# Two output projections as 2x2 block products by multiplication, with their weights' sums made by accumulating transfers

## The chip, the cores and the metric

The kernel runs on one NeuronCore of one Trainium2 chip. It is one program for five engines with an instruction queue each: TensorE (PE in the profile; its weight loads are PEld), VectorE (DVE), ScalarE (ACT), GpSimd (POOL) and SyncE (SP). Sixteen DMA engines move data between the chip's DRAM and the core's on-chip memory; in this kernel SP issues most transfers and POOL the rest. The metric is the device time of one execution in microseconds (us), given as the median of the runs.

## The reference, cut to what matters

An encoder layer is applied to two sequences of 1024 rows, `x_prompt` (b = 0 below) and `x_sample` (b = 1), all widths 1024:

```python
xn = rmsnorm(x, g_pre)
fv, fg, hv, hg, mg = split(xn @ w_in)           # 1024, 1024, 3*1024, 1024, 2*1024 columns
fz  = fftn(fv by groups).real
y_f = (fz * silu(fg)) @ w_fourier_out           # the F projection
z   = two long convolutions by FFT, gated, of short_conv(hv)
y_h = (z * silu(hg)) @ w_hyena_out              # the H projection
g_f, g_h = split(sigmoid(mg + b_merge))
out = (g_f * y_f + g_h * y_h) @ w_out
y   = x + rmsnorm(out, g_post)
```

The change concerns `y_f`, `y_h` and how their gated sum reaches the product with `w_out`.

## The kernel before

**Pairs.** A float32 number x is kept as a pair of rounded numbers h + l. `split` (L167) makes one: ScalarE casts x to h (L170) and VectorE, or POOL in places, subtracts h from x (L180). A product of pairs is three matmuls, h·h, h·l and l·h (`mm3`, `times`; all at L193). One matmul takes a 128x128 left factor and a 128x512 right factor.

**Stages.** `phase_fourier` (0 to about 200 us of the span) norms both inputs, spills the normed x to DRAM as `d_x` (L360) and does the Fourier branch. `phase_main` makes the filters' spectra (to about 700 us) and calls `branches` (L1030, to about 1677 us): per column tile `conv`, `conv_front`, `conv_back`, all of b = 0 before all of b = 1. `inproj` (L836) is its matmul with a 128-column tile of `w_in`: it loads 512 columns of weights at a time on SP, splits them with POOL (`wl<-wr,wh`, with two buffers for the raw weights and three for a pair), and for b = 0 keeps the pairs in DRAM by POOL's queue (`d_w`) so that b = 1 can load them. `load_x` (L823) loads a sequence's normed x in 8 tiles of 512 KB and splits each 1024 wide; it runs for b = 1 at about 1090 us. Ten gates of b = 1 (list `PLAIN`) are done plainly at the end of the stage.

`phase_gates` (L1118, 1677 to 1884 us) makes the other gates of b = 1 in 11 jobs. A job is two column tiles, that is a 2x2 block product done with seven products instead of eight (Winograd's form): the left factors are blocks 11, 12, 22 and sums s1 to s4 of the weights, the right factors blocks B11, B21, B22 and sums T1 to T4 of x. Each of the seven products is 12 matmuls (4 k-tiles of three). Results go to DRAM as `d_g`.

`phase_out` (L1230, 1884 to 2235 us) does F and H in four units, a unit being half of the rows of one sequence. A unit runs `project` (L1269) for F over 8 output tiles `dt` and then for H over 8: 24 matmuls each into one PSUM bank, with the left factor from `weight` (L1255), which loads 128x512 weights on POOL's queue (`wr<-in_w_fo`, `wr<-in_w_ho`) and splits them, again in each unit. `operand` loads the right factors (`sf`, `sh`), `gated` (L1288) multiplies a result by a sigmoid gate (L1293) loaded from `d_g`. F's gated results stay on chip (`yf`); H's are added to them and the sum is stored as `d_m` (L1377), in an order that later lets a 128x512 block be read in one piece. `beside` splits `w_out` and its sums between the units, half of the sums by way of DRAM (`d_t`).

`last_rows` (L1388, 2235 us to the end) multiplies `d_m` by `w_out` in 8 jobs of seven products, with the same Winograd form, norms the rows, adds x and stores y.

**What sets the order.** Each engine runs its own queue in order. A scheduler orders each queue; an instruction that depends on nothing may be moved far ahead of where it is written. `issue_after(i)` keeps what is written under it behind instruction i. Data that the program writes to DRAM and reads back, and buffers that rotate, are tracked: a reader waits for the transfer that wrote it, and a new use of a buffer for the last use of the old one.

Of the kernel before, what the change touches and what calls it, by code (L numbers as in the profile page):

```python
# [9 lines left out]
F32 = mybir.dt.float32  # L10
# [6 lines left out]
P = 128  # L17
D = 1024
# [142 lines left out]
class K:  # L161
# [34 lines left out]
    def setup(self, ctx):  # L196
# [29 lines left out]
        self.d_m = [dt(f"d_m{u}", [P, 4, 8, P]) for u in range(2 * NB)]  # L226
        self.d_t = [dt(f"d_t{j}", [P, 4, 512]) for j in range(2)]
# [595 lines left out]
    def load_x(self, b, ks=range(8)):  # L823
        nc = self.nc
        if 0 in ks:
            self.xh, self.xl = [], []
        for k in ks:
            h = self.xp.tile([P, L], F32R, tag=f"xh{k}", name=f"xh{b}_{k}", bufs=1)
            l = self.xp.tile([P, L], F32R, tag=f"xl{k}", name=f"xl{b}_{k}", bufs=1)
            r = l.bitcast(F32)  # L830
            nc.sync.dma_start(r, self.d_x[b][k])
            self.split(h, l, r, "dve", "act")
            self.xh.append(h)
            self.xl.append(l)

    def inproj(self, sec, mt, b=None):  # L836
# [3 lines left out]
        for q in range(2):  # L840
# [5 lines left out]
            if b:  # L846
                for t, k in zip(parts, kept):
                    nc.sync.dma_start(t.bitcast(F32), k[:, s])
            else:
                r = self.wp.tile([P, 512], F32, tag="w", name="wr", bufs=2)  # L850
                nc.sync.dma_start(r, a["w_in"][sec, mt][:, s])
                self.split(*parts, r, "pool", "act")
                if kept:
                    for t, k in zip(parts, kept):
                        nc.gpsimd.dma_start(k[:, s], t.bitcast(F32))
            for n in range(2):
                for kk in range(4):
                    k = 4 * q + kk
                    s = slice(512 * n, 512 * n + 512)
                    self.mm3(ps[:, s], (h[:, kk], l[:, kk]), (self.xh[k][:, s], self.xl[k][:, s]), k == 0, k == 7)  # L860
# [122 lines left out]
    def phase_main(self, nct=8, nb=NB, nf=16):  # L983
        tc, nc, a = self.tc, self.nc, self.a
        with ExitStack() as es:
# [19 lines left out]
            nc.gpsimd.tensor_copy(self.cfwd[:, 0, 0:1], self.xl[4][:, 0:1])  # L1005
# [6 lines left out]
            for i in range(nf):  # L1012
# [11 lines left out]
                if i in (2, 4, 6):  # L1024

                    s = slice((2, 4, 6).index(i) * INVW // 3, ((2, 4, 6).index(i) + 1) * INVW // 3)
                    nc.gpsimd.dma_start(self.cinv[:, :, s], a["c_inv"][:, :, s])
            self.branches(nb, nct, ws)

    def branches(self, nb, nct, ws):  # L1030
# [13 lines left out]
        def front(i):  # L1044
            b, n, c = steps[i]
# [72 lines left out]
    def phase_gates(self):  # L1118

        tc, nc, a = self.tc, self.nc, self.a
        wp, b = self.wp, 1
        jobs = [(s, c) for c in range(0, 8, 2) for s in (0, 4, 5, 6) if (s, c) not in self.PLAIN]
        with ExitStack() as es:
            pool = lambda n: es.enter_context(tc.tile_pool(name=n, bufs=1, reuse_waits="tile"))
            self.open_mm(es, "psg")
            gs, gw, gr = pool("gs"), pool("gw"), pool("gr")
            def prepare(sec, c):


                r = gr.tile([P, 4, 512], F32, tag="raw", name="wraw", bufs=2)
                for i in range(2):
                    nc.gpsimd.dma_start(r[:, 2 * i:2 * i + 2].rearrange("p a b -> p (a b)"), a["w_in"][sec, c + i])
                s = gw.tile([P, 4, 512], F32, tag="sum", name="wsum", bufs=1)
                A = {}

                def parts(n, pool, tags, src, bufs):
                    h, l = [pool.tile([P, 4, P], F32R, tag=t, name=t, bufs=bufs) for t in tags]
                    self.split(h.rearrange("p a b -> p (a b)"), l.rearrange("p a b -> p (a b)"), src, "dve", "act")  # L1140
                    A[n] = h, l
                parts("11", wp, ("wh", "wl"), r[:, 0], 3)
                parts("12", wp, ("wh", "wl"), r[:, 1], 3)
                self.add("dve", s[:, 0:2], r[:, 2].unsqueeze(1).to_broadcast([P, 2, 512]), r[:, 3::-3])
                self.add("dve", s[:, 2], s[:, 0], r[:, 0])
                parts("s2", gw, ("s2h", "s2l"), s[:, 2], 1)
                h, l = [gw.tile([P, 2, 4, P], F32R, tag=t, name=t, bufs=1) for t in ("s13h", "s13l")]
                f = lambda t: t.rearrange("p s a b -> p s (a b)")
                self.split(f(h), f(l), s[:, 0:2], "dve", "act")
                A["s1"], A["s3"] = (h[:, 0], l[:, 0]), (h[:, 1], l[:, 1])  # L1150
                self.add("dve", s[:, 3], s[:, 2], r[:, 1])
                parts("s4", gw, ("s4h", "s4l"), s[:, 3], 1)
                parts("22", gw, ("a2h", "a2l"), r[:, 3], 1)
                return A

            A = prepare(*jobs[0])
            TH, TL = [], []
            for k in range(4):
                r = gr.tile([P, 4, 512], F32, tag="raw", name="xraw", bufs=2)
                for i in range(2):  # L1160
                    nc.sync.dma_start(r[:, 2 * i:2 * i + 2].rearrange("p a b -> p (a b)"), self.d_x[b][k + 4 * i])
                s = gw.tile([P, 4, 512], F32, tag="sum", name="xsum", bufs=1)
                self.sums(s, r)
                h, l = [gs.tile([P, 4, 512], F32R, tag=f"{t}{k}", name=f"{t}{k}", bufs=1) for t in ("th", "tl")]
                self.split(h, l, s, "dve", "act")
                TH.append(h)
                TL.append(l)
            own = lambda k, n: (slice(0, 512), slice(512, 1024))[n]
            block = lambda i, n: [(self.xh[4 * i + k][:, own(k, n)], self.xl[4 * i + k][:, own(k, n)]) for k in range(4)]
            B11, B21, B22 = block(0, 0), block(1, 0), block(1, 1)  # L1170
            T1, T2, T3, T4 = [[(TH[k][:, j], TL[k][:, j]) for k in range(4)] for j in range(4)]

            def out(sec, c, n, p, q, op):

                s = slice(512 * n, 512 * n + 512)
                t = wp.tile([P, 512], F32, tag="gt", name="gt", bufs=3)
                if q is not None:
                    self.tt("dve", t, p, q, op)
                if sec in (0, 4):
                    f = gw.tile([P, 512], F32, tag="f", name="fz", bufs=3)  # L1180
                    nc.sync.dma_start(f, (self.d_sh if sec else self.d_fz)[b][c][:, s])
# [4 lines left out]
                nc.sync.dma_start(self.d_g[b][sec][c][:, s], t)  # L1186

            def kept(p, own=False, last=False):
                if own or last:
                    t = gw.tile([P, 512], F32, tag="u" if own else "f", name="u" if own else "v", bufs=1 if own else 3)  # L1190
                else:
                    t = wp.tile([P, 512], F32, tag="w", name="m", bufs=2)
                copied = nc.scalar.copy(t, p)
                if own:
                    self.copied = copied
                return t

            def first(A):
                pa, pb = self.psum("mm", 4, "pg"), self.psum("X", 2, "pg")
                self.times(pa, A["11"], B11, True)  # L1200
                m1 = kept(pa)
                self.times(pb, A["12"], B21, True)
                return pa, pb, m1
            pa, pb, m1 = first(A)
            for i, (sec, c) in enumerate(jobs):
                out(sec, c, 0, pb, m1, ADD)
                self.times(pa, A["s2"], T2, False)
                u = kept(pa, True)
                pc = self.psum("T", 2, "pg")
                self.times(pc, A["s3"], T3, True)  # L1210
                self.times(pa, A["s1"], T1, False)
                v = kept(pa, last=i + 1 == len(jobs))
                out(sec, c + 1, 1, pc, v, SUB)
                last = (A, pa, pc, u)
                if i + 1 < len(jobs):
                    A = prepare(*jobs[i + 1])
                    pa, pb, m1 = first(A)
                A_, pa_, pc_, u = last
                if i + 1 < len(jobs):
                    self.times(pa_, A_["s4"], B22, False)  # L1220
                    out(sec, c, 1, pa_, None, None)
                else:
                    pd = self.psum("X", 2, "pg")
                    self.times(pd, A_["s4"], B22, True)
                    out(sec, c, 1, pd, v, ADD)
# [392 lines left out]
```

## Time and profile before

| | us |
|---|---|
| runs | 2398.54, 2398.01, 2397.57 (median 2398.01) |
| profiled execution, span from first to last instruction | 2394.9 |
| F and H projections (`pyf`, `pyh`) on the chain | 1884 to 2235.5 |
| gates (`pg`) on the chain | 1677 to 1884 |
| last rows (`po`) | 2235.5 to the end |

The median of the runs is 3.1 us above the span of the profiled execution. The profile gives each engine's busy time, the chain of waits (from the last instruction back to whatever released each step), groups of equal instructions with count, busy time and mean, and the transfers with the time from issue to landing. In a group's line, `out<-in` names the tiles, and what follows the last bar is the engine's idle time just before these instructions and what ended it.

### The profile page before, as it was taken

What the parts mean: (1) busy time and instruction counts of PE and PEld (TensorE: products, weight loads), DVE (VectorE), ACT (ScalarE), POOL (GpSimd) and SP (SyncE); (2) the same over time, 40 slices, a digit from 0 to 9 for tenths busy, and PEclk for the clock granted to TensorE, in tenths of its full rate; (3) what the DMA queues carried; (4) which work ended last, traced back from release to release, by engine and by line L of the source; (5) the groups of instructions that cost most, each with busy time, mean ns of one, the idle gap of its engine ahead of it and who ended that gap; (6) DMA issues with size and microseconds to landing.
All of it is one profiled execution on the core that took longest, in us unless ns stands there. A gap on an engine that the chain in (4) does not pass through costs nothing.

```text
span 2394.9 us, 36369 instructions
## 1 busy us (share of the span) xinstructions
PE 2360.9 (99%) x12988; PEld 2053.6 (86%) x12988; DVE 1889.5 (79%) x3397; ACT 1084.2 (45%) x2063; POOL 461.6 (19%) x506
## 2 busy tenths in 40 slices
PE   6999999999999999999999999999999999999998
PEld 5998888888888888888888888888888888888887
DVE  7875787888879999999989999985555456665677
ACT  6654666677643333333322223333443445444444
POOL 3341222222232233230000000023000111112111
PEclk9999999999999999999999999999999999999999
DMA  8636655555665555545444444435544667776553
GB/s 264 219 129 220 204 169 165 171 171 159 204 215 177 172 170 187 176 145 203 150 131 133 137 150 133 143 121 198 165 160 141 211 215 259 251 259 213 166 166 132
DMA packets 221007, 428.33 MB, mean 179 GB/s; under 512 B 23254, under 2 KB 80952, under 8 KB 220570
## 3 DMA queue, kind: packets, MB, share of 16 engines
q1 hardware_dynamic: 193037, 333.03, 43.1%
q0 software_dynamic: 27568, 92.94, 11.5%
q8 instruction: 102, 1.67, 0.3%
q14 instruction: 79, 0.65, 0.1%
q10 hardware_dynamic: 221, 0.04, 0.0%
HBM read 290.12 MB, written 135.79 MB: 178 GB/s over the span
## 4 chain that ended last, share of the span: by engine, by line
PE 94%; DVE 2%; DMA 1%; ACT 1%; issue 1%; POOL 0%; DVEq 0%; ACTq 0%; POOLq 0%; SPq 0%
PE pin L193 41%; PE pg L193 8%; PE pyf L193 7%; PE pyh L193 7%; PE pX L193 7%; PE pT L193 7%; PE po L193 6%; PE pXf L193 3%; PE pfv L193 3%; PE pft L193 1%; PE tph L901 1%; DVE eo L180 0%; PE pQ L193 0%; DMA wr<-in_w_fo 0%; PE pse L193 0%
## 5 line engine op out<-in xcount | busy, mean ns | idle before, releaser
L193 PE MATMUL pin<-xh,wl 128*128 128x512 f32 x1440 | 563.2, 391 | 0.0
L193 PE MATMUL pin<-xl,wh 128*128 128x512 f32 x1440 | 562.8, 391 | 0.1
L193 PE MATMUL pin<-xh,wh 128*128 128x512 f32 x1440 | 561.9, 391 | 0.0
L180 POOL TENSOR_TENSOR wl<-wr,wh 128x512 fp32r<-128x512 f32 x132 | 227.6, 1725 | 1148.7 <-ACT wh L170 1125.4
L193 PEld LDWEIGHTS pin<-xl,wh 128*128 128x128 f32 x1440 | 271.0, 188 | 50.8 <-DVE xl L180 0.4
L193 PEld LDWEIGHTS pin<-xh,wh 128*128 128x128 f32 x1440 | 270.8, 188 | 51.0
L193 PEld LDWEIGHTS pin<-xh,wl 128*128 128x128 f32 x1440 | 271.0, 188 | 50.5
L170 ACT CAST wh<-wr 128x512 fp32r<-128x512 f32 x260 | 161.1, 620 | 333.6 <-PE pin L193 107.8
L180 DVE TENSOR_TENSOR t<-pX,k 128x1024 f32<-128x1024 f32 x128 | 155.6, 1216 | 9.8 <-PE pX L193 6.5
L193 PE MATMUL pX<-bh,cfwd 128*128 128x256 f32 x768 | 162.3, 289 | 0.0
L180 DVE TENSOR_TENSOR wl<-wr,wh 128x512 fp32r<-128x512 f32 x128 | 87.9, 688 | 91.5 <-ACT wh L170 91.5
L193 PE MATMUL pyf<-sf,wh 128*128 128x512 f32 x512 | 157.7, 389 | 0.0
L193 PE MATMUL pyh<-sh,wh 128*128 128x512 f32 x512 | 157.4, 389 | 0.0
L193 PE MATMUL pT<-cinv,yh 128*128 128x256 f32 x768 | 145.3, 284 | 0.0
L193 PEld LDWEIGHTS pT<-cinv,yh 128*128 128x128 f32 x768 | 123.2, 190 | 6.8
L170 ACT CAST bh<-b 128x512 fp32r<-128x512 f32 x144 | 89.1, 620 | 87.3 <-DVE b L180 50.6
L193 PEld LDWEIGHTS pX<-bh,cfwd 128*128 128x128 f32 x768 | 126.4, 190 | 2.2
L193 PEld LDWEIGHTS pyf<-sf,wh 128*128 128x128 f32 x512 | 96.1, 188 | 20.0
L193 PEld LDWEIGHTS pyh<-sh,wh 128*128 128x128 f32 x512 | 96.1, 188 | 20.0
L193 PE MATMUL pT<-cinv,yl 128*128 128x256 f32 x384 | 109.0, 284 | 0.0
L193 PE MATMUL pX<-bl,cfwd 128*128 128x256 f32 x384 | 108.9, 284 | 0.0
L170 ACT CAST yh<-y 128x512 fp32r<-128x512 f32 x96 | 59.4, 619 | 100.9 <-DVE y L180 98.0
(384 smaller groups left out, 5340.6 us busy)
## 6 DMA issues: line engine op xcount, KB each, us to landing
k<-d_k SPq DMA_DIRECT2D x128, 512.0 KB, 4.1
wr<-in_w_in SPq DMA_DIRECT2D x132, 256.0 KB, 3.2
d_g<-gt SPq DMA_DIRECT2D x124, 256.0 KB, 2.6
d_k<-kt SPq DMA_DIRECT2D x128, 128.0 KB, 2.2
d_k<-kt SPq DMA_DIRECT2D x64, 256.0 KB, 2.3
wr<-in_w_fo POOLq DMA_DIRECT2D x64, 256.0 KB, 4.0
g<-d_g SPq DMA_DIRECT2D x64, 256.0 KB, 4.2
wr<-in_w_ho POOLq DMA_DIRECT2D x64, 256.0 KB, 3.9
```

The costliest lines, as they stand in the source:

```text
L170: self.rounded = nc.scalar.copy(h, src)
L180: return e.tensor_tensor(out, a, b, op=op)
L193: return self.nc.tensor.matmul(out, lhsT, rhs, start=start, stop=stop, skip_group_check=shared)
L901: nc.tensor.transpose(tp[:, q * P:(q + 1) * P], eo[:, e, q], self.ident)
```

## The change

- `phase_gates`, `phase_out` and `last_rows` become one function, `phase_tail`. F and H are now four nets, (F, b=0), (H, b=0), (F, b=1), (H, b=1), each a whole 1024x1024x1024 product in 2x2 blocks: 7 products x 4 column tiles = 28 steps of 12 matmuls. Gates and last rows remain jobs of seven products.
- The right factors of a net are made on VectorE from loads of the gated input; they live in four rooms, T2, T3, T1, T4, which rotate, and in the cells of x. The seven left factors of each weight, sums included, lie ready in DRAM (`d_s`).
- `weight_sums` makes `d_s` with 22 transfers of 1 MB from DRAM to DRAM on POOL's queue, 8 of them accumulating. `front` issues two for each i from 2 to 12, all in the part of `branches` that works on b = 0.
- F's gated result is stored to `d_m` by SP; H's is added to it in DRAM by an accumulating transfer on POOL's queue. `d_m` has rows of 2 KB now, and the last rows' loads read 512-byte pieces of it.
- `w_out`'s sums are made in four of the gates' jobs (`last_sums`, three operations of POOL and one of VectorE each) and go by way of DRAM (`d_t`); its own blocks are copied from DRAM to DRAM (`d_wo`) and loaded from there in the last steps.
- Every instruction of a net has its step in a table (`at`), and is issued behind what ScalarE and VectorE were last given (`pinned`, `step`).
- `load_x` makes 16 half tiles, with transfers of 256 KB and splits 512 wide.
- In the order of instructions that results, the 8 copies into `d_wo` stand as the 12th to 17th and the 21st and 22nd transfers of SP's queue, at the start of the kernel; the first eight `d_x` stores stand behind them.

```diff
 def load_x(self, b, ks=range(8)):
...
+            for n in range(2):
+                t = self.xp.tile([P, 2, 512], F32R, tag=f"x{n}{k}", name=f"x{n}{b}_{k}", bufs=1)
+                r = t[:, 1].bitcast(F32)
+                nc.sync.dma_start(r, self.d_x[b][k][:, 512 * n:512 * n + 512])
+                self.split(t[:, 0], t[:, 1], r, "dve", "act")
...
         def front(i):
+            with tc.issue_after(self.pooled.ins):
+                for f in self.sums_due[max(2 * i - 4, 0):max(2 * i - 2, 0)]:
+                    f()
...
+    def weight_sums(self):
+        nc, a = self.nc, self.a
+        out = []
+        for n, w in enumerate(("w_fo", "w_ho")):
+            v = a[w].rearrange("(j i) p (h c) -> i h p j c", i=2, h=2)
+            d = self.d_s[n]
+            load = lambda p, src, d=d: out.append(lambda: nc.gpsimd.dma_start(d[p], src))
+            more = lambda p, src, d=d: out.append(lambda: nc.gpsimd.dma_start(d[p], src, accum_op=ADD))
+            load(0, v[0, 0])
+            load(1, v[0, 1])
+            load(6, v[1, 1])
+            load(3, v[1, 0])
+            more(3, v[1, 1])
+            load(5, v[1, 0])
+            more(5, v[0, 0])
+            load(2, d[3])
+            more(2, v[0, 0])
+            load(4, d[2])
+            more(4, v[0, 1])
+        return out
+
+    def phase_tail(self):
...
+            def load_r(n, q):
...
+                R[n, q] = t
+                d = self.d_g[b][0] if nm == "f" else self.d_g[b][4] if b else self.d_sh[b]
+                for k in range(4):
+                    nc.sync.dma_start(piece(t, k), d[4 * (q // 2) + k][:, 512 * (q % 2):512 * (q % 2) + 512])
+            def sum_r(n, i, last):
+                r = [halves(R[n, q])[i] for q in range(4)]
+                if last:
+                    self.add("dve", r[2], r[3], r[2])
+                    return
+                self.sub("dve", r[0], r[0], r[1])
+                self.sub("dve", r[1], r[1], r[3])
+                self.stt("dve", r[3], r[0], -1.0, r[3], MUL, SUB)
+            def block(g, i):
...
+                if i == 0:
+                    blocks[g] = gs.tile([P, 2, 4, 512], F32R, tag=ROOM[(g - 1) % 4], name="n", bufs=1)
+                t = blocks[g]
+                self.split(t[:, 0, 2 * i:2 * i + 2], t[:, 1, 2 * i:2 * i + 2], halves(r)[i], "dve", "act")
...
+            def load_w(i):
...
+                nc.sync.dma_start(flat(l).bitcast(F32), flat(self.d_s[n % 2][p][:, i % 2 * 2:i % 2 * 2 + 2]))
+            def weight(i):
+                h, l = W[2 * i]
+                self.split(flat(h), flat(l), flat(l).bitcast(F32), "dve", "act")
...
+            def net_out(s, p, q, op2):
+                nm, b = nets[s // 28]
+                c, m, o = out_of(s)
+                t = wp.tile([P, 512], F32, tag="gt", name="gt", bufs=3)
+                if q is not None:
+                    self.tt("dve", t, p, q, op2)
+                self.mul("dve", t, p if q is None else t, G[s])
+                dst = self.d_m[2 * b + m][:, c]
+                if nm == "f":
+                    nc.sync.dma_start(dst, t)
+                else:
+                    nc.gpsimd.dma_start(dst, t, accum_op=ADD)
+            def product(s):
+                n, p, j = s // 28, s % 28 // 4, s % 4
...
+                self.times(t, W[s], blocks[s // 4], p in (0, 1, 5))
...
+            for n in range(len(nets)):
+                z, early = 28 * n, n == 0
+                at(z - (7 if early else 12), load_r, n, 0)
+                at(z - (6 if early else 6), load_r, n, 2)
+                at(z - (3 if early else 10), load_r, n, 1)
+                at(z - (3 if early else 12), load_r, n, 3)
+                for i in range(2):
+                    at(z + i + 0.5, sum_r, n, i, False)
+                    at(z + 2 * i + 4, sum_r, n, i, True)
+                at(z + 7, load_r, n, 3)
+            for i in range(END // 2):
+                s = 2 * i
+                at(s - 7 if i > 3 else (-6, -6, -6, 2)[i] if i < 4 else 2, load_w, i)
+                at(s - 4 if i != 3 else 3.2, weight, i)
+            for s in range(END):
+                if out_of(s):
+                    at(s - 5, load_g, s)
+                    at(s - 2, open_g, s)
+            for g in range(END // 4):
+                for i in range(2):
+                    at(4 * g + (-6, -6, -5, -5, -5, -10, -10)[g % 7] + 2 * i, block, g, i)
...
+            for k in range(8):
+                nc.sync.dma_start(self.d_wo[k], a["w_out"][k * P:(k + 1) * P])
```

More of the change, by code (lines that the diff above doesn't have):

```diff
@@ new lines, in phase_tail @@
+            for s in range(2, END):
+                pinned(product, s)
+                step(s)
+            A = ahead[-1]
+            Y = {j: pairs(z) if j[0] == "B" else quad(z) for j, z in Z.items()}
+            pa, pb, m1 = first(A, Y)
+            for k in range(2):
+                round_z("T3", k)
+            load_sum("T1")
+            with tc.issue_after(self.copied.ins):
+                list(prep)
+                for k in range(2):
+                    round_z("T1", k)
+                for k in range(4):
+                    round_z("B22", k)
```

651 lines of the change are left out of this document (314 added, 337 removed).

## The prediction, made before the changed kernel was run

> **What bounds the kernel now.** I read first the page's busy shares and its chain of waits, then the chain piece by piece from the gates on, then TensorE's waits, then busy time by stage.
>
> ```profile
> span 2394.9 us, 36369 instructions
> PE 2360.9 (99%) x12988; PEld 2053.6 (86%) x12988; DVE 1889.5 (79%) x3397; ACT 1084.2 (45%) x2063; POOL 461.6 (19%) x506
> ...
> PE 94%; DVE 2%; DMA 1%; ACT 1%; issue 1%; POOL 0%; DVEq 0%; ACTq 0%; POOLq 0%; SPq 0%
> ```
>
> TensorE is busy in 99% of the span, and 94% of the chain that ends last is its own work. So matmuls that go away are worth their full time, unless TensorE then has to wait. The pieces of the chain give the price of one.
>
> ```profile
> 1890.53 40.35 PE pyf L193 x178
> 1930.88 43.52 PE pyh L193 x192
> 1974.40 43.52 PE pyf L193 x192
> ...
> 2192.00 43.52 PE pyh L193 x192
> 2235.52 149.61 PE po L193 x660
> ```
>
> A unit of the F or H projection (8 output tiles of 24 matmuls) takes 43.52 us for 192 matmuls, eight times over with no gap: 43.52/192 = 0.2267 us each. The stage's 1536 matmuls are 348.2 us, from about 1884 to 2235.5.
>
> ```profile
> PE pXf L193 <- ACT kt L810: 1.7, 1, 1.7
> PE pT L193 <- ACT xt L902: 0.8, 1, 0.8
> PE pg L193 <- ACT u L1193: 0.4, 1, 0.4
> PE pX L193 <- DVE b L180: 0.4, 1, 0.4
> ```
>
> Those are all of TensorE's waits between 200 and 2240 us: 3.3 us. There is nothing to win there and much to lose. How much cover the other engines have shows by stage (columns: length, PE, PEld, DVE, ACT, POOL busy, clock, DMA share, GB/s).
>
> ```profile
> 800.00:1240.00 440.00, 438.76 (x2611) 389.18 (x2610) 419.97 (x675) 151.81 (x268) 89.14 (x85) 1.00 0.52 167
> 1676.00:1884.00 208.00, 207.55 (x915) 171.39 (x915) 116.65 (x166) 84.08 (x142) 12.73 (x25) 1.00 0.48 159
> 1930.00:2060.00 130.00, 130.00 (x575) 107.63 (x575) 81.19 (x123) 61.92 (x102) 25.48 (x48) 1.00 0.75 245
> ```
>
> VectorE is at 62% and the DMA engines at 0.75 in the F and H stage; VectorE is at 95% in the first half of the branches.
>
> **What is removed.** A projection of a sequence, now called a net, is 2x2 blocks by seven products: 28 steps of 12 matmuls = 336, against 2 x 192 = 384 before. Four nets: 1344 against 1536, so 192 matmuls go: 192 x 0.2267 = -43.5 us. The order and size of one matmul (128x512, three for a product of rounded pairs) are as before, and the gates (11 jobs) and the last rows (8 jobs) keep theirs. Also gone are 128 weight loads with their 128 casts and 128 subtractions, and POOL's issues of them; none of that is on the path now.
>
> **What the nets ask of the engines.** A step is 12 x 0.2267 = 2.72 us, a net 76.2 us.
>
> ```profile
> L180 DVE TENSOR_TENSOR xl<-xl,xh 128x1024 fp32r<-128x1024 f32 x16 | 19.4, 1218 | 2.8 <-ACT xh L170 2.7
> L170 ACT CAST xh<-xl 128x1024 fp32r<-128x1024 f32 x16 | 16.6, 1051 | 3.8 <-DMA xl<-d_x 3.5 <-PE pin L193 0.3
> L180 DVE TENSOR_TENSOR yf<-pyf,g 128x512 f32<-128x512 f32 x32 | 22.1, 690 | 23.1 <-PE pyf L193 21.2 <-ACT g L1293 1.9
> L1293 ACT ACTIVATE g<-g,bm 128x512 f32<-128x512 f32 x64 | 46.2, 721 | 18.2 <-DMA g<-d_g 17.1 <-DVE wl L180 1.0
> L1193 ACT COPY m<-pg 128x512 f32<-128x512 f32 x21 | 12.2, 581 | 1.4 <-PE pg L193 1.4
> ```
>
> VectorE per net: 14 weight pieces and 14 right-hand pieces to split and 8 sums, all 1024 wide, 36 x 1.218 = 43.8 us; 16 gate products and 12 joins of 512, 28 x 0.690 = 19.3 us; together 63.2 us, 83% of the net where 62% was. ScalarE: 28 x 1.051 + 16 x 0.721 + 12 x 0.581 = 47.9 us, 63%. Both fit beside TensorE in the mean. At a change of net the sums and the next room's splits come together: about 24 us of VectorE work in eight steps (21.8 us), so a wait of up to 3 us at each of four starts is possible, and none if rows overlap. The sums wait for loads issued 6 to 12 steps ahead (16 us or more), longer than any landing shown below.
>
> DMA per net: right factors 20 x 256 KB, weights 14 x 512 KB, gates and results 16 x 256 KB each: 21 MB in 76.2 us, 275 GB/s, against 245 at share 0.75 in the row above. An H net also accumulates into F's result; if that reads 4.2 MB more, it is 331 GB/s. What this core reaches shows in its first 30 us, in 40 slices:
>
> ```profile
> GB/s 0 0 63 277 317 374 377 376 394 415 412 379 396 405 413 415 421 404 410 408 402 396 196 33 0 89 264 38 334 233 305 148 262 351 108 160 330 334 327 374
> ```
>
> About 400 GB/s hold for ten microseconds, so 331 fits with little to spare. In the Trainium skill, "DMA: Bandwidth & Descriptors", section "Where 436 GB/s comes from", HBM gives one core some 358 GB/s; by that an H net would stand at 331/358, or 92%, and queues would lengthen. The row's 421 lies above it, so the trace doesn't bear the rule out on plain loads.
>
> **The accumulating results.** The trace has no such transfer. Its nearest rows are a store of 256 KB on POOL's queue and one on SP's; a gate's load and the longest landing stand with them:
>
> ```profile
> d_w<-wl POOLq DMA_DIRECT2D x27, 256.0 KB, 5.2
> ...
> g<-d_g SPq DMA_DIRECT2D x48, 256.0 KB, 4.2
> ...
> d_m<-yf SPq DMA_DIRECT2D x24, 256.0 KB, 3.8
> ...
> t1l<-d_t SPq DMA_DIRECT2D x1, 1024.0 KB, 8.5
> ```
>
> A result sits in one of three gt buffers until its transfer has landed. In the last three products of an H net a result is due every step, 12 in a row; a buffer comes round after 3 x 2.72 = 8.16 us, of which VectorE's two operations take 1.4. Landing in up to 6.8 us costs nothing. What is queued behind a late one is VectorE's join, and behind it on that engine the splits that TensorE needs next. I take 5.2 us, the POOL store: nothing. At twice that (a read and a write one after the other), 10.4 us, each result is (10.4 + 1.4 - 8.16)/3 = 1.2 us late, 12 of them 14.6 us, less some 5 us of lead: 9 to 10 us per H net, 19 in all. At three times, 15.6 us, 12 x 2.95 - 5 = 30 per net, 60 in all. From below nothing can be gained: the store of before delayed nobody.
>
> F's results are stored by SP. Each store waits for VectorE's product, and behind it on SP's queue stand the loads of weights and gates; those are issued 7 and 5 steps (19 and 13.6 us) ahead, three times the 4.2 us of a gate's landing, so a store that is a step late still costs nothing; with that lead gone, a late gate load would hold VectorE's product as an accumulate does. The rows of d_m are now written 2 KB wide and read back in 512-byte pieces, a job's two loads of 512 KB under seven products (19 us): nothing, against 8.5 us for twice one such load in the row above; an unhidden load would cost that once a job.
>
> In the Trainium skill, same page, "Rules for kernel authors", an accumulating transfer reads its destination and writes it later. No run shows one yet. By that the bytes are those I counted, and a landing nearer 10.4 than 5.2 gives the 19 us above; it is the doubt in my term.
>
> **The weight sums.** Twenty-two transfers of 1 MB from DRAM to DRAM (8 accumulating) go out on POOL two at a time in the first half of the branches. They move 23 MB, 31 with the accumulates' reads, over some 400 us: 58 to 78 GB/s on top of 167, and the share goes from 0.52 to 0.70 or 0.76, what the F and H stage has now. POOL's queue holds four places where a transfer waits for the one just ahead of it, and behind it wait POOL's subtractions of weights, which TensorE needs:
>
> ```profile
> POOL wl L180 <- ACT wh L170: 179.3, 29, 10.0
> ```
>
> POOL itself idles up to 10 us for a cast there, and two weight buffers ahead are 2 x 24 x 0.2267 = 10.9 us. A 1 MB transfer at the 8.5 us of the row above, in the middle of that, costs 0; at twice it, 17 - 11 = 6 us at each of four places. I take +1, bounds 0 and +24, nearer the low end since the row itself fits. The extra traffic may also make filter rows (512 KB each) land later than TensorE's 1 us of wait now shows; it is in the same bound.
>
> **The copies of w_out.** Written in the tail, they depend on nothing, and the order of instructions puts all 8 of 512 KB on SP's queue at the very start: six behind the x loads, two just ahead of the first stores of normalised x (d_x), with the second pair of wfv loads and all of d_x queued behind them. The place where that can tell is early on the chain of waits:
>
> ```profile
> 34.99 8.10 DMA d_x<-xg
> ```
>
> The round trip of the last d_x store stands on the chain for 8 us, so what delays those stores moves everything behind.
>
> The copies move 4.2 MB: 10.5 us at 0.4 MB a us. The stretch 16.5 to 20 us shows idle DMA in the slices above (33, 0, 89 GB/s), so a part is free. Bounds 0 and +10.5; I take +4, the middle less that gap. The x tiles split in halves add 8 subtractions a load, 8 x (2 x 0.690 - 1.218) = 1.3 us of VectorE, hidden behind the branches' matmuls, or 1.3 if the cover (5% there) is gone.
>
> **Gates into nets, nets into rows.** The first net's loads, gates of the last job and sums of w_out (POOL and VectorE, in a stage at 56% VectorE) share eight steps; at the other end the last right factor of w_out is loaded into a room that is free only with the last net's last steps and is wanted four products, 10.9 us, later: landing 4 to 5, cast 1.05, subtraction 1.2, twice, some 9.5 us. I take +5 for both and the four net starts, bounds 0 and +15.
>
> **The sum.** -43.5 (matmuls) + 4 (copies) + 1 (sums in the branches) + 0 (accumulating results) + 5 (starts of nets and rows) = -33.5 us. On the span: 2394.9 - 33.5 = 2361.4; the median of the runs is 3.1 us above the span, so 2364.5.
>
> **Rivals.** (a) All is hidden: -43.5, or 2354.5. For it: the same seven products run in the gates with 0.4 us of wait. Against it: VectorE at 83% and the copies at the start. (b) The added work shows in part: the copies pay 10.5, accumulating results land in 10.4 us (19), starts of nets 8, branches 1: -43.5 + 38.5, near 2393; with half of the accumulates' price, 2383. For it: no row shows an accumulate. (c) Slower: accumulating results land so late that the three buffers run dry. The place is the last three products of both H nets, the price 8 x (T - 6.8) - 10 us in all from T = 8 us on (12/3 x 2 nets), and with +10 elsewhere the gain is gone at T = 12.2 us; at 15.6 it is +60 + 10 - 43.5, about 2425. For it: the queue of POOL is in software and DMA is at its fullest there. Against it: at 256 KB the rows' landings stand at 3.8 to 5.2 under share 0.75. (d) The change does not do what it says: the matmuls stay but TensorE is paced by VectorE in all nets. At 63.2 of 76.2 us it would need 20% more than its rows; a net at 80 us is +15, beside the other terms 2380.
>
> **Chances.** Forecast with its neighbourhood (2357 to 2372) 0.45; (a) 0.12; (b) and (d), 2372 to 2393, 0.20; around the old time 0.05; (c) 0.18. The likeliest case alone spans 2357 to 2373; the range has to reach into (b) and the mild end of (c): 2352 to 2405, with about 0.13 above. This kernel's measurement tells nothing under 0.2% (4.8 us) from no change. So faster 0.77, same 0.05, slower 0.18.
>
> **What would show it.** Right: a matmul count lower by 192, chain pieces of 12 matmuls or more in a row at 0.2267, TensorE's waits in the nets under 5 us in sum, landing of accumulating transfers near 5 us, VectorE at 80 to 85% between the gates and the rows. Wrong: a wait of TensorE on a split whose VectorE queue waits for an accumulating transfer (c); waits at every net's first steps on sums (d); the first net matmul more than 10 us later than now because of the start or of the branches; POOL's subtractions released by DMA. The forecast falls if TensorE waits for more than 20 us in all.

## The result and the profile after

The changed kernel takes 2380.8 us (median of 4 runs, 2379.2 to 2382.4) against 2398.2 of before: ratio 0.9924, 95% interval 0.991 to 0.9938, or 17.4 us less. The forecast was 2364.5 in a range from 2352 to 2405. The matmuls went as counted; about 60% of the 43.5 us that they save is spent elsewhere.

The page of the changed kernel's profiled execution (that run took 2382.25 us):

```profile
span 2380.5 us, 36106 instructions
PE 2330.1 (98%) x12796; PEld 2022.8 (85%) x12796; DVE 1973.3 (83%) x3416; ACT 1115.5 (47%) x2083; POOL 430.7 (18%) x406
...
PE 52%; DVE 3%; DMA 3%; issue 1%; ACT 0%; SPq 0%; DVEq 0%; POOL 0%; POOLq 0%; ACTq 0%
```

The last line is the chain of waits. It is followed back only to 957 us here, so its shares add up to 59% of the span and can't be set against the 94% of before. The span with the mean granted clock of TensorE (0.998 before):

```profile
core 0: 2380.5 us, clock 0.994
```

12988 - 12796 = 192 matmuls fewer. But TensorE's busy time fell by 2360.9 - 2330.1 = 30.8 us, not by 43.5: the matmuls that are left took 12.7 us longer, and its idle time grew from 34.0 to 50.4 us. The two make the 29.1 us between the saving of 43.5 and the span's 14.4.

Where they lie, matched points of the two programs show (first and last start of a tile's matmuls; columns: least, median and longest ns, then the two starts in us). First before, then after:

```profile
L193 PE MATMUL pin<-xh,wh x1440: 387/389/485, 199.1 to 1676.3; 128*128 128x512 f32 x180
L193 PE MATMUL pX<-b,cfw x256: 270/275/377, 702.7 to 1599.1; 128*128 128x128 f32 x128
L193 PE MATMUL pg<-xh,wh x88: 389/389/389, 1676.9 to 1866.7; 128*128 128x512 f32 x88
```

```profile
L193 PE MATMUL pin<-x,wh x2880: 387/389/481, 203.8 to 1688.0; 128*128 128x512 f32 x192
L193 PE MATMUL pX<-b,cfw x256: 270/275/377, 709.4 to 1616.0; 128*128 128x128 f32 x128
L193 PE MATMUL pg<-x,wh x176: 389/389/500, 1689.8 to 1886.8; 128*128 128x512 f32 x176
```

The first in-projection (`pin`) starts 4.7 us later; the first `pX` of the branches 6.7 later, so the filters added 2.0; the first gate matmul (`pg`) 12.9 later, so the branches added 6.2. The rest, some 16 us, is behind that point. TensorE's waits after 200 us name it:

```profile
PE pg L193 <- ACT m L1215: 3.7, 1, 3.7
PE pg L193 <- DVE wl L180: 3.4, 1, 3.4
PE pin L193 <- ACT ktmp L794: 2.4, 1, 2.4
PE pX L193 <- DVE b L180: 2.2, 2, 1.8
PE pn L193 <- DVE wl L180: 1.5, 1, 1.5
PE pg L193 <- ACT gt L885: 1.2, 1, 1.2
```

The first line is in the gates (1695.6 us), the second and fifth at the passage from the last net to the rows (2217.0 and 2201.6). Behind the two long ones the clock of TensorE is at half, and matmuls start 0.43 us apart instead of 0.227 (busy time by stretch: length, then busy time and count of TensorE, its weight loads, VectorE, ScalarE and POOL, then granted clock, DMA share and GB/s):

```profile
1698.60:1705.40 6.80, 6.13 (x14) 4.78 (x15) 6.80 (x11) 2.88 (x7) 1.59 (x1) 0.50 0.92 295
2220.80:2224.20 3.40, 3.40 (x10) 2.63 (x9) 3.31 (x7) 1.80 (x3) 0.86 (x1) 0.50 1.00 128
```

TensorE works for 6.1 us of the first and 3.4 us of the second, so half speed costs 3.1 and 1.7. The gates then lose 3.7 + 3.1 and the rows 1.5 + 3.4 + 1.7. The nets themselves ran dense, with TensorE at 277.88 of 278 us, VectorE at 80% and the DMA engines at 0.87:

```profile
1912.00:2190.00 278.00, 277.88 (x1225) 229.47 (x1224) 223.59 (x240) 167.21 (x217) 19.29 (x23) 1.00 0.87 276
```

The chain of waits has them in two pieces. Between these it runs over VectorE and two accumulating transfers of the first H net, which TensorE did not have to wait for:

```profile
1923.28 103.22 PE pn L193 x454
2082.52 118.22 PE pn L193 x520
```

The last 2 us are at the very end, where the last rows' x comes late (chain of waits: start, length, what):

```profile
2367.45 5.57 DMA xr<-in_x
2373.14 1.42 DVE o L176 x2
```

Each run below tests a theory A, that one of these losses has a cause of its own (the copies of w_out, the traffic of the weights' sums, too few buffers for accumulating results, or rooms that come free late), against a rival that is named with it, for instance that accumulating transfers load the DMA engines far beyond their bytes, or that the new order of instructions is to blame. Times are medians with the kernel before on the same chip (2398.1, 2398.0 and 2396.9 in three groups); the interval of each ratio is about 0.0013 (3 us) either way, so differences under 4 us are read from the profile, not from the medians. A profile is that of one execution, and half-speed stretches come and go between executions (last section).

### The profile page after: what moved, and what is told of

It is laid out like the page before. It is cut to its first block, busy times and chain, and to the rows that moved or that the text cites. A ratio compares the mean times of both kernels' runs of the same rounds, so it can differ in the third digit from the quotient of the medians.

```text
span 2380.5 us, 36106 instructions
## 1 busy us (share of the span) xinstructions
PE 2330.1 (98%) x12796; PEld 2022.8 (85%) x12796; DVE 1973.3 (83%) x3416; ACT 1115.5 (47%) x2083; POOL 430.7 (18%) x406
## 4 chain that ended last, share of the span: by engine, by line
PE 52%; DVE 3%; DMA 3%; issue 1%; ACT 0%; SPq 0%; DVEq 0%; POOL 0%; POOLq 0%; ACTq 0%
PE pin L193 17%; PE pg L193 14%; PE pn L193 10%; PE pT L193 5%; PE pX L193 5%; DMA d_m<-gt 1%; PE tph L904 1%; DMA xraw<-d_x 1%; DMA d_sh<-x 0%; DVE gt L180 0%; DMA g<-d_g 0%; DVE T L180 0%; DVE wl L180 0%; DVE xraw L180 0%; DVE r L180 0%
## 5 line engine op out<-in xcount | busy, mean ns | idle before, releaser
L193 PE MATMUL pin<-x,wh 128*128 128x512 f32 x2880 | 909.8, 391 | 2.5 <-ACT ktmp L794 2.4
L193 PEld LDWEIGHTS pin<-x,wh 128*128 128x128 f32 x2880 | 534.3, 188 | 103.4 <-ACT ktmp L794 2.6
L193 PE MATMUL pin<-x,wl 128*128 128x512 f32 x1440 | 563.2, 391 | 0.0
L193 PEld LDWEIGHTS pin<-x,wl 128*128 128x128 f32 x1440 | 271.0, 188 | 50.8
L193 PE MATMUL pn<-n,wh 128*128 128x512 f32 x896 | 276.4, 389 | 0.1
L193 PEld LDWEIGHTS pn<-n,wh 128*128 128x128 f32 x896 | 168.1, 188 | 35.8 <-DVE n L180 0.5
L193 PE MATMUL pn<-n,wl 128*128 128x512 f32 x448 | 174.6, 390 | 1.6 <-DVE wl L180 1.5
L180 DVE TENSOR_TENSOR bl<-b,bh 128x512 fp32r<-128x512 f32 x144 | 101.5, 709 | 0.5 <-ACT bh L170 0.5
L193 PEld LDWEIGHTS pn<-n,wl 128*128 128x128 f32 x448 | 84.1, 188 | 19.7 <-DVE wl L180 2.5
L180 DVE TENSOR_TENSOR y<-t 128x512 f32<-128x512 f32 x128 | 91.8, 717 | 5.4 <-PE pT L193 4.9
```

Of the source, the lines that this page charges most:

```text
L180: return e.tensor_tensor(out, a, b, op=op)
L193: return self.nc.tensor.matmul(out, lhsT, rhs, start=start, stop=stop, skip_group_check=shared)
```

## The experiments

**The copies of w_out later.** `kload` is the load of k issued last.

```diff
 def front(i):
...
+            if 18 <= i < 26:
+                with tc.issue_after(self.kload.ins):
+                    nc.sync.dma_start(self.d_wo[i - 18], self.a["w_out"][(i - 18) * P:(i - 17) * P])
...
-            for k in range(8):
-                nc.sync.dma_start(self.d_wo[k], a["w_out"][k * P:(k + 1) * P])
```

> The copies of w_out into d_wo go behind k loads in the part of branches that works on b = 1, one each, instead of the start. Theory A (the copies hold up the first stores and loads): the first in-projection matmul comes at 199 us again instead of 203.8, the half-speed stretch at 43 us goes, and the time falls by 4 to 5 us, to about 2376. Rival (the start is late because the scheduler ordered it otherwise, not because of the copies): the first in-projection matmul stays at 203 to 204 and the time within 1 us of 2380.8. If the branches then pay for the copies, part of the gain comes back as waits after 1100 us.

2375.4 us, 22.7 under before (the changed kernel: 17.4). The first in-projection is back:

```profile
L193 PE MATMUL pin<-x,wh x2880: 387/389/477, 199.5 to 1681.4; 128*128 128x512 f32 x192
```

199.5 us against 203.8: theory A, with 4.3 us in this pair of traces. All the traces together give less. With the copies at the start the first in-projection begins at 200.0 to 204.1 us (seven traces, median 202.7; the 200.0 is the run with the pinned sum below), with the copies moved at 199.5 to 200.7 (four traces, median 200.0). So the copies cost some 3 us, and one execution with them at the start lost nearly nothing. The half-speed stretch at 43 us is gone, but one of the same length stands at 32 to 40 us.

**Without the weights' sums.** `weight_sums` keeps `load(0, v[0, 0])` of each net; `load_w` reads that for every factor.

> Only 2 of the 22 transfers of weight_sums are left (the nets load one block for every left factor, so y is not the reference's). Theory A (the 22 MB from DRAM to DRAM, and POOL waiting for them, delay the filter rows k and POOL's splits): TensorE's 4.0 us of idle time between 700 and 1100 us fall below 1, k lands in 4.1 us again instead of 5.0, and the time falls by 4 to 6 us, to about 2376. Rival (the branches are longer because of the half tiles of x and the new order of instructions): idle time stays at 3 us or more and the time within 1.5 us of 2380.8.

2371.3 us, 26.8 under before. TensorE has no wait at all between 700 and 1100 us. From the first `pX` to the first gate matmul it takes 974.1 us, as before the change (974.2). Theory A, with a gain larger than it allowed: 6.3 us are the branches, 1.1 the start and 3.6 what stands behind the first gate matmul. The four traces with the sums where the change put them have 980.4 to 982.7 us for the branches, so this loss is not chance. But this run can't tell traffic from accumulating.

**The same 22 transfers, none of them accumulating.**

```diff
-            more = lambda p, src, d=d: out.append(lambda: nc.gpsimd.dma_start(d[p], src, accum_op=ADD))
+            more = lambda p, src, d=d: out.append(lambda: nc.gpsimd.dma_start(d[p], src))
```

> The 8 accumulating transfers of weight_sums are plain copies of the same size at the same places (the left factors are then no sums, so y is not the reference's). Theory A (traffic and POOL's queue set the price in the branches, not the accumulating): at least two thirds of the branches' loss stay, first gate matmul at 1687 us or later, time 2377 to 2381. Rival (accumulating is what costs, by its reads and its longer landing): the first gate matmul comes at 1684 us or earlier and the time falls by 5 us or more, to 2376 or below.

2375.3 us, 22.7 under before, and the first gate matmul at 1682.7: the rival.

```profile
L193 PE MATMUL pg<-x,wh x176: 388/389/500, 1682.7 to 1879.5; 128*128 128x512 f32 x176
```

From the first `pX` it is 973.9 us, as without any sums. So 21 MB of plain copies, and POOL waiting for them (33.0 us in six places between 700 and 1100 us, against 50.0 in seven in the changed kernel), are hidden; that 8 of the transfers accumulate costs all of the 6 us. What they do shows in the share of the DMA engines' time that POOL's queue takes between 700 and 1100 us (packets, MB, share), first with accumulating, then with plain transfers, then without the sums:

```profile
q0 software_dynamic: 13177, 42.84, 35.1%
```

```profile
q0 software_dynamic: 10991, 42.31, 28.3%
```

```profile
q0 software_dynamic: 6527, 21.37, 13.3%
```

The 20 plain copies of 1024 KB in this stretch take 15.0% of 400 us, or 60 us of all sixteen engines: 3.0 us each. With 8 accumulating ones among them it is 21.8%, 27 us more: by this estimate some 6.4 us for an accumulating one, 2.1 times a plain one. The DMA engines' share goes to 0.73, and rows that VectorE needs come late (`k` lands in 5.0 us, against 4.3 in the same stretch before the change). VectorE's waits for them, with accumulating and with plain transfers:

```profile
DVE t L180 <- DMA k<-d_k: 5.9, 3, 3.4
```

```profile
DVE t L180 <- DMA k<-d_k: 1.6, 1, 1.6
```

Before the change and without the sums there is no such wait here. All of TensorE's waits in this stretch of the changed kernel (3.9 us) end with VectorE and none with POOL, so POOL's longer waits are not what reached it.

**The sums in the filters.** The 22 go out one or two per filter step from step 2 on, and in an order in which none stands directly behind the one it needs.

> The 22 transfers of weight_sums go out one or two per step of the filters (200 to 700 us) instead of two per step of the branches, and no transfer stands directly behind the one it waits for. Theory A (in the branches their traffic delays the filter rows k, which VectorE and then TensorE wait for; the filters read no such rows): TensorE's idle time between 700 and 1100 us falls from 4.0 us to below 1, the filters lose under 2 us, and the time falls by 6 to 9 us, to about 2373, near what leaving 20 of the transfers out gave (2371.3). Rival (the transfers cost the same wherever they run): the filters become 5 us or more longer and the time stays within 2 us of 2380.8.

2384.8 us, 13.2 under before, 4 worse than the changed kernel: the rival, and worse than it said. The branches are as short as without sums (973.8 us), but the filters lose 13 (first `pX` at 722.2). TensorE was busy for 488 of 500 us in them where the changed kernel has 497, with the DMA engines at 0.72:

```profile
200.00:700.00 500.00, 488.15 (x2645) 421.86 (x2644) 398.52 (x881) 322.06 (x687) 148.40 (x108) 1.00 0.72 221
```

Which late transfer holds up the filters was not followed.

**The sums beside b = 1.** The plain transfers on SP behind k loads, the accumulating ones on POOL, two per step, in the order of the last run:

```diff
 def front(i):
...
+            if i >= 17:
+                for f in self.sums_due[2 * i - 34:2 * i - 32]:
                     f()
...
+            def load(p, src, d=d):
...
+                    with self.tc.issue_after(self.kload.ins):
+                        nc.sync.dma_start(d[p], src)
...
+            def more(p, src, d=d):
...
+                    with self.tc.issue_after(self.pooled.ins):
+                        nc.gpsimd.dma_start(d[p], src, accum_op=ADD)
```

> The 22 transfers of weight_sums go out in the part of branches that works on b = 1, two per step: the 14 plain ones on SP behind k loads, the 8 accumulating ones on POOL, which has next to nothing else to do there. The DMA engines' share is 0.45 there, against 0.55 before any sums in the part on b = 0. Theory A (the accumulating transfers hold the DMA engines about twice as long for their bytes, which costs where the engines are already busy and POOL's splits queue behind them): the part on b = 0 is as long as before the change, the part on b = 1 loses under 2 us, the first gate matmul comes 976 us or less after the first pX, against 980.4, and the time falls by 4 to 7 us, to 2374 to 2377. Rival (they cost the same anywhere, as in the filters, where they cost 12 us): time 2380 or more.

2371.2 us, 25.7 under before: theory A, and a better time than it expected, with the full result kept. From the first `pX` to the first gate matmul: 975.1 us. The gates got shorter too: from their first matmul to the first of product s4 it takes 21.1 us against 26.1 in the changed kernel, and none of their matmuls takes over 0.5 us, so there is no half-speed stretch. Why is not shown. The place decides: here the DMA engines' share rises from 0.45 to only 0.59,

```profile
1100.00:1640.00 540.00, 538.83 (x3208) 478.45 (x3207) 497.49 (x820) 163.46 (x299) 34.30 (x22) 1.00 0.59 189
```

and accumulating transfers of 1024 KB that land in 13.5 and 18.7 us (medians of the two weights) hold nobody up; POOL is busy for 34 of 540 us. Whether the lower share, the idle POOL or the plain copies on SP matters most, this run doesn't separate.

**Plain stores of H's results.** `net_out` without `accum_op`.

> The H nets store their results plainly on POOL's queue instead of accumulating them (F's part is lost from d_m). Theory A (accumulating transfers land in 7.2 us, over the 6.8 us that three buffers leave, and hold VectorE up where the rows begin): landing falls to about 5 us, the two waits at 2201 and 2217 us (1.5 and 3.4 us) and the half-speed stretch behind them go, and the time falls by 5 to 7 us, to about 2375. Rival (the right factors of w_out come late into a room that is free only at the end): the waits stay and the time falls by less than 1.5 us.

2375.8 us, 22.3 under before. The long wait at the rows is the one below, another is 0.5 us, and no half-speed stretch stands there; landing falls from 7.2 to 5.1 us:

```profile
PE pg L193 <- DVE wl L180: 0.8, 1, 0.8
```

```profile
d_m<-gt POOLq DMA_DIRECT2D x31, 256.0 KB, 7.2
```

```profile
d_m<-gt POOLq DMA_DIRECT2D x32, 256.0 KB, 5.1
```

Size and sign are as theory A said; whether three buffers are the reason was left to the next run. In nine other traces after the change this wait is 3.2 to 5.1 us long.

**Five buffers for the last results.**

```diff
+                if s >= 104 and s % 2:
+                    t = cell(xp, "x06" if s % 4 == 1 else "x07", "gx")[:, 0]
```

> In the last eight steps of the last net every second result goes to one of two cells of x that are free there, so five buffers rotate instead of three; the transfers accumulate as before. Theory A (three buffers are too few for a landing of 7.1 us): the waits at 2201 and 2217 us fall from 5 us to under 2, the half-speed stretch behind them goes, and the time falls by 3 to 5 us, to 2376 to 2378, as with plain stores (2375.8). Rival (what costs is that accumulating transfers load the DMA engines and delay w_out's factors): the waits stay above 3 us and the time within 1.5 us of 2380.8.

2380.8 us, 17.2 under before: the rival. VectorE waits for accumulating results for 0.4 us now, but TensorE's waits at the rows are still 3.2 and 0.6 us. What VectorE waits for instead shows in the changed kernel already (2150 to 2225 us):

```profile
DVE wsum L180 <- DMA wraw<-d_m: 5.5, 1, 5.5
DVE wl L180 <- ACT wh L170: 2.0, 2, 1.5
DVE gt L180 <- DMA d_m<-gt: 1.8, 3, 0.9
```

A sum for the rows' second job stands at the head of VectorE's queue for 5.5 us until its load of d_m lands; with five buffers that is 4.4 us, with plain stores 2.3. The DMA engines are full there (share 1.02 from 2195 to 2222 us, 0.75 with plain stores).

**That sum behind the last net.**

```diff
+            ended = newest(dve)
...
+                    with tc.issue_after(ended):
                         A = prepared("o", *rows[i + 1])
```

> One thing is changed: the operations that prepare the second job of the last rows may not stand on VectorE ahead of the last net's last instruction. In the changed kernel its first sum stands there at 2193 us and waits 5.5 us for a load of d_m, and everything of the last net queues behind it. Theory A (this wait at the head of VectorE's queue, made long by the busy DMA engines, is what TensorE pays for at the rows): VectorE's wait goes, TensorE's waits at 2201 and 2217 us fall from 4.9 us to under 1.5, no half-speed stretch stands behind them, and the time falls by 4 to 6 us, to 2375 to 2377. Rival (VectorE has too much to do there, and the wait only fills a gap): TensorE's waits stay above 3 us, the time within 2 us of 2380.8.

2380.4 us, 16.5 under before: by time, the rival. By the profile, half of theory A: the wait for the load is gone and so is TensorE's at 2201 us, and the passage has no half-speed stretch, but VectorE now waits 3.8 us for accumulating results, and TensorE 3.3 us at the same matmul as before:

```profile
DVE gt L180 <- DMA d_m<-gt: 3.8, 4, 1.6
DVE oT L180 <- ACT oT L170: 2.3, 2, 1.8
```

With one wait taken away another takes its place, while plain stores shorten both. That five buffers and the pinned sum together would end it was not tried. The missing half-speed stretch can be chance: in the last run below, with the same edit, one follows this wait.

**Rooms for the gates' x.** Every second load of x goes into two cells (`st0`, `st1`) instead of a raw room; the load of `gp` is held back too.

> Every second load of x for the gates' right factors goes into two spare cells instead of the two raw rooms, so that a load does not wait for the splits of the one before. Theory A (sums made in place keep a raw room until the last of four splits, so loads come every 12 us): TensorE's waits of 1.2 and 3.7 us at 1689 to 1699 us and the half-speed stretch of 6.8 us behind them go, and the time falls by 6 to 8 us, to about 2374. Rival (the room becomes free too late from the branches, first load at 1648 us instead of 1626): at least 3 us of wait stay and the time falls by under 3 us.

2380.1 us (2377.7 to 2387.8), 18.0 under before. By the conditions set beforehand this is the rival: 1.5 + 1.6 = 3.1 us of wait stay, and the time falls by 0.6 us. But no half-speed stretch follows these waits, so that the gates lose some 5 us less in that execution (1.2 + 3.7 + 3.1 in the changed kernel):

```profile
1690.00:1706.00 16.00, 14.43 (x63) 11.59 (x63) 10.22 (x11) 4.98 (x9) 9.02 (x7) 1.00 1.00 351
```

In the changed kernel a load of x waits for VectorE's splits of an earlier one (SP's waits from 1600 to 1700 us), and the chain in the gates reads

```profile
SPq L1513 <- DVE T L180: 10.7, 3, 6.0
```

```profile
1686.61 7.88 DMA xraw<-d_x
1694.59 1.82 DVE xraw L180
1696.43 1.66 DVE xraw L176
1698.11 0.62 ACT T L170
```

So sums made in place are a likely part of the cause of the gates' wait; the load of `gp`, held back by the same edit, is not told apart from them.

**Edits together.** Four (`all_four`): late copies, sums in the filters, rooms for x, five buffers. Three (`best_nox`): late copies, sums beside b = 1, pinned sum. The three and the rooms for x (`best`).

> The late copies of w_out, the sums in the filters, spare cells for the gates' x and for the last net's results, together. Theory A (four separate costs that add): 4.7 us at the start, 7 in the branches, 5 in the gates, 4 at the rows; the time falls by 17 to 21 us to 2360 to 2364, within 6 to 10 us of the matmuls' own saving (2398.2 - 43.5 = 2354.7). Rival (the stages hand waits on to each other, and half-speed stretches come back elsewhere): 2366 to 2372.

> Late copies of w_out, sums in the part on b = 1, and the pinned preparation of the rows' second job, together. Theory A (the three costs add): 5 + 5 + 5, 2364 to 2368. Rival (they hand waits on to each other, as the four together did, 2382.1): 2372 or more.

> As the run with three of the edits, and every second load of x for the gates in spare cells. Theory A: the waits of 1.2 and 3.7 us at the gates' start shrink to 3 us in all without a half-speed stretch behind them, 3 to 5 us under the run with three, 2360 to 2364. Rival (as alone, where the gates began better by the profile and the median did not move): within 1.5 us of the run with three.

The four: 2382.1 us, 15.9 under before, worse than theory and rival; the filters lost 17 us this time (from the first `pin` to the first `pX` it took 522.2 us, against 505.6 in the changed kernel) and took all. The three: 2374.8 us, 22.0 under, the rival; no better than the sums beside b = 1 alone (25.7). The copies now share that stretch with them, with a wait of 2.2 us at 1368 us that the sums alone did not have, and the gates' wait came back (2.4 us). With the rooms for x: 2369.5 us (2368.4 to 2373.0), 27.4 under before, ratio 0.9887 (0.9873 to 0.99), 10 us better than the change as it was made. That is 5.4 us under the three, so the step is theory A's, though the level is not; the gates' waits are 1.5 and 1.0 us and no half-speed stretch follows. It is the lowest time of all, but the 1.7 us to the sums beside b = 1 alone are within the interval. What is left of its waits:

```profile
PE pg L193 <- DVE wl L180: 4.2, 1, 4.2
PE pin L193 <- ACT ktmp L794: 2.4, 1, 2.4
PE pT L193 <- DVE yl L180: 1.8, 1, 1.8
```

## Why the prediction was right, and where it was off

The time fell as forecast, and for the reason given: 192 matmuls fewer, in nets that run dense. But of the 33.5 us that the sum promised 17.4 came. The terms against the saving, 10 us in the sum, are 28 us in the trace: 4.7 at the start, 2.0 in the filters, 6.2 in the branches, 6.8 in the gates, 6.6 at the rows and 2.0 at the end. The range holds the result because it was drawn wide for rivals. And one of the signs that the prediction gave for being wrong came true: the first net matmul starts at 1900.8 us instead of 1884.5, more than 10 us later.

- **The matmuls, -43.5.** Right in count and in price; the nets ran dense. The clock was taken as constant, though: mean clock 0.994 against 0.998. The new half-speed stretches cost 3.1 us in the gates and 1.7 at the rows; at the start there are 10.2 us at half speed instead of 3.4. These are contained in the 28 us above; no term of the sum had them.
- **The copies of w_out, +4 (0 to 10.5).** The in-projection starts 4.7 us later in the changed kernel's trace and 3.6 later in the median of seven traces; moving the copies brought back 2.7 between medians. Right in place and size.
- **The sums in the branches, +1 (0 to 24).** Mis-sized: 6.2 in the branches. I priced the bytes and POOL's waits behind transfers of 8.5 us, at four places; plain copies of the same size are hidden, POOL's waits with them. What costs is accumulating: a transfer then takes about 2.1 times a plain one's time on all sixteen engines. I had allowed for the read in the bytes, and saw the share reach 0.76 (it was 0.73), but took a share that the F and H stage bears to be harmless here, where VectorE is at 95% and its waits for late rows of `k` reach TensorE.
- **Accumulating results, 0 at a landing of 5.2 us.** Landing was 7.2, between my two ends and just over the 6.8 that I worked out as free; VectorE waited for accumulating results 9.0 us in all, and TensorE lost nothing to it in the first H net. In the last net plain stores gave 5 us back. The mechanism that I named, too few buffers, is not enough for that: more buffers alone gave nothing, and nor did the pinned sum alone. The Trainium skill's "DMA: Bandwidth & Descriptors", section "Rules for kernel authors", has an accumulating transfer read its destination and write it later. The double engine time agrees with that.
- **Starts of nets and rows, +5 (0 to 15).** The four starts of nets cost nothing. The rows cost 6.6 in the trace, by VectorE waiting in order for a load and for results, not by the last right factor, which I named. That the size is near is luck.
- **The gates, 0.** That the gates run on as before was wrong: their first load of x went out at 1648 instead of 1626 us, and sums of x in place kept the next loads waiting, so that TensorE waited 3.7 us and then worked 6.1 us at half speed: 6.8 us. That is the largest term that I missed.
- **Filters and end, 0.** 2.0 us each; the wait of 2.4 us for `ktmp` stands in nine traces after the change, with and without the transfers moved, and not in the one before, so no moved transfer caused it. What did was not tried.

By number rival (d), 2380, came closest, but by luck: TensorE was not paced by VectorE in the nets. In kind it was (b), that the added work shows in part (2383 to 2393), though with other terms; (c), that the accumulates run the buffers dry, was not what happened.

## What to carry to other kernels

An accumulating transfer is to be priced by the DMA engines' time (here about twice a copy's for its bytes), and issued where those engines and the issuing queue are idle: the same 22 transfers cost 13 us in the filters, 6 beside b = 0 and about 1 beside b = 1. A kernel in which TensorE never waits has no slack in its clock either: waits of 3.4 and 3.7 us cost 5 and 7 in the changed kernel's trace. And an instruction that a scheduler moved ahead on an in-order engine holds up whatever queues behind it when its load is late. To judge a change of a few microseconds, look at the same point in several traces: the start alone moved by 4 us between runs that have it in common.

## What the runs showed of the hardware

Half-speed stretches follow short waits, and not each time. The same wait of 2.4 us in the filters was followed by full speed in the changed kernel and by half in the run with the pinned sum (13 us, the last 2.2 of them behind the wait, and in the other run the 3.3 us behind it):

```profile
672.00:685.00 13.00, 10.57 (x57) 8.95 (x56) 12.36 (x26) 7.48 (x15) 4.96 (x6) 1.00 0.71 225
```

```profile
678.90:682.20 3.30, 3.21 (x8) 2.57 (x9) 3.30 (x8) 0.73 (x2) 0.00 (x0) 0.50 0.37 150
```

In eight traces with this wait, half speed follows it in four. In the run with the pinned sum a wait of 1.8 us at 935 us was followed by 3.4 us at half, too, while its wait of 3.3 us at the rows was followed by full speed. The Trainium skill's "TensorE: Matmul & The Clock Gate", section "What's actually happening", puts the fall after an idle window of about 3.4 us. Here less idle time was enough, and the stretches behind these waits were 3.4 or 6.8 us long. It may also be why executions after the change lie wider apart than those of before (2377.7 to 2387.8 in the run with rooms for x, 2395.7 to 2399.8 for all of before), which hid gains of 5 us that the profiles show.
